# Conditioning projections in four column groups; the linear attention's two directions issued in pairs

## The chip, the cores and the metric

The kernel runs on one core of one Trainium2 chip. The metric is device time of one execution in microseconds. The kernel before took 5521.72 us as the median of three runs (5514.61 to 5526.49).

## The reference

One inference step of a two-layer backbone of width 1024, for 128 context tokens and 512 latent tokens. Each layer has a token mixer and then an expert channel mixer, and each of these is modulated by vectors that come from a conditioning vector:

```
mod = silu(cond) @ ada_w + ada_b            # (2 conditionings, 6 * 1024): shift1, scale1, gate1, shift2, scale2, gate2
h   = x * (1 + scale1) + shift1
x   = layer_norm(ALPHA * x + gate1 * token_mixer(h))
h   = x * (1 + scale2) + shift2
x   = layer_norm(ALPHA * x + gate2 * peer(h))
```

The token mixer runs grouped attention beside a gated linear attention, which scans the tokens in chunks of 64, once forward and once backward, in four heads, with a 128 x 256 state S:

```
def step(S, inp):                            # one chunk of one direction of one head
    o     = A @ v + q_e @ S                  # 64 x 256
    S_new = exp(b_last) * S + (k * exp(b_last - b)).T @ v
```

The context has two chunks and starts from zero states, the latents have eight and start from given ones. The expert mixer (`peer`) picks 128 of 16384 rows of two tables for each token by product keys.

## The kernel before, in words

One core does everything. The program is written as Python generators that trace instructions; `merge` and `weave` interleave two tracks by hand-written costs: the latent track (`s_mixer(0)`, `s_peer(0)`, `s_mixer(1)`, `s_peer(1)`) and the context track (`p_mixer`, `p_front`, `p_peer` for each layer). The framework's planner then fixes the order of the instructions on each engine when the program is built: it takes the traced order as priority and simulates when operands and buffers come free. On the chip each engine follows its fixed order and waits on semaphores; all plain transfers of weights are issued by SP, the expert gathers by GpSimd.

*Conditioning.* `ada(l, vs, W)` makes the vectors `vs` of layer l for both conditionings at once. It is called three times: alone at the very start for shift1 and scale1 of layer 0 (`p_ada(0)`); inside the context mixer of layer 0 for the other four (`mixer`, with the mixer's own four weight buffers); and for all six vectors of layer 1 (`p_ada(1)`) woven with the context gathers of layer 0. The weights of one vector are 1024 x 1024. They are read in four column tiles of 256 columns, each in two transfers of 512 KB (`Weights.__call__`, line 129). For each tile, eight products of fp32, `csil` (128 x 2, stationary) with 128 x 256 weights (moving), accumulate in rows 0 and 1 of a PSUM tile `modr` (line 151); each product is two matmul instructions. Then VectorE copies `modr` to `mr` (line 169), and two transposes (line 161) turn `mr` into columns of `modp`, one tile later. PSUM has two banks under the tag `mm0`, of which `modp` holds one for a whole vector and `modr` the other. `p_ada(0)` has 12 weight buffers of 512 KB, `p_ada(1)` has 2. After the first two tiles `p_ada` calls `layer_params`, which issues small transfers.

*Linear attention.* `gates(h)` prepares the operands of head h, `scan(h)` runs its two directions. In each step the loop of lines 454 to 474 goes through direction 0 and then direction 1, each in its own chunk: the product with the state, `o` (line 461: stationary 128 rows x 64 columns, so 64 of the array's columns, in the half that the chunk's place decides); the state's increment, `kv` (line 466: stationary 64 rows x 128 columns, so 64 of the array's rows, in the half that the chunk's place decides), into one of two PSUM banks (`mm0` for the context, `mm1` for the latents); and the update of S on VectorE (line 471, or 469 where S was zero). Since the step's two chunks are n and last - n, the two directions always use opposite halves. The latents' last step has no `kv`, the context's first step no `o`.

Of the kernel before, what the change touches and what calls it, by code (L numbers as in the profile page):

```python
# [7 lines left out]
F32 = mybir.dt.float32  # L8
# [10 lines left out]
L = 2  # L19
D = 1024  # L20
ND = D // 128
SP, SS, PAST = 128, 512, 256
H, G, HD = 16, 4, 64
GH, DK, DV = 4, 128, 256
# [7 lines left out]
CW = 256  # L32
# [31 lines left out]
def kernel(ctx: ExitStack, tc, xp, xs, ck, cv, st, cond, adaw, adab, win, wglr,  # L64
                              nrm, w2, gb, gn, wao, wgo, wout, lnp, wq, sk, pu, put, pv, rope, cst, msk,
                              yp, ys, nk_out, nv_out, ns_out):
    nc = tc.nc
# [23 lines left out]
    def psm(name, tr=0):  # L91
        return ps.tile([128, 512], F32, tag=f"mm{tr}", bufs=2, name=name)
# [21 lines left out]
    csil = consts.tile([128, ND, 2], F32, name="csil")  # L114
# [6 lines left out]
    class Weights:  # L121
        def __init__(self, pool_, split, bufs):
            self.pool, self.split, self.bufs = pool_, split, bufs

        def __call__(self, src):
            raw, h, lo = [], [], []
            for i in range(2):
                r = self.pool.tile([128, 4, CW], F32, tag="w", bufs=self.bufs, name="w")
                nc.sync.dma_start(r, src[:, 4 * i:4 * i + 4, :])
                raw.append(r)  # L130
                if not self.split:
                    continue
                wh = self.pool.tile([128, 4, CW], F32R, tag="wh", bufs=3, name="wh")
                nc.scalar.activation(wh, r, AF.Copy)  # L134
                wl = self.pool.tile([128, 4, CW], F32R, tag="wl", bufs=3, name="wl")
                (nc.vector, nc.gpsimd)[i].tensor_sub(wl, r, f32(wh))  # L136
                h.append(wh)
                lo.append(wl)
            if not self.split:
                return [lambda j: raw[j // 4][:, j % 4, :]]  # L140
            return [lambda j: h[j // 4][:, j % 4, :], lambda j: lo[j // 4][:, j % 4, :]]
# [6 lines left out]
    def accumulate(out, mk):  # L148
        n = len(mk)
        for i, (lt, rt) in enumerate(mk):  # L150
            nc.tensor.matmul(out, lt, rt, start=(i == 0), stop=(i == n - 1))  # L151

    def ada(l, vs, W):
        p = lp[l]
        for v in vs:
            mp = psm("modp")
            m3 = mp[:, 0:2 * ND].rearrange("p (c s) -> p c s", s=2)

            def turn(t, mr):
                for k in range(2):  # L160
                    nc.tensor.transpose(m3[:, 2 * t + k, :], mr[:, k * 128:(k + 1) * 128], ident[0:2, 0:2])

            late = None
            for t in range(4):
                w = W(adaw[l, 4 * v + t])
                rp = psm("modr")
                accumulate(rp[0:2, 0:CW], [(csil[:, j, :], w[0](j)) for j in range(ND)])
                mr = lay.tile([2, CW], F32, tag="mr", bufs=2, name="mr")
                nc.vector.tensor_copy(mr, rp[0:2, 0:CW])
                if late:  # L170
                    turn(*late)
                late = t, mr
                yield 3.5
            turn(*late)
            mod = lay.tile([128, ND, 2], F32, tag=f"mod{v}", bufs=2, name="mod")
            nc.vector.tensor_add(mod, m3, p["adb"][:, ND * v:ND * v + ND, None].to_broadcast([128, ND, 2]))
            if v in (SCALE1, SCALE2):
                nc.vector.tensor_scalar(mod, mod, 1.0, None, op0=OP.add)
            elif v == GATE1:
                nc.vector.tensor_scalar(mod, mod, 0.5, None, op0=OP.mult)  # L180
            p["mod", v] = mod
            if v in (SHIFT1, SCALE1):
                continue
            rp = psm("rowp")
            nc.tensor.transpose(rp[0:2 * ND, 0:128], mod.rearrange("p c s -> p (c s)"), ident)
            rows = lay.tile([2 * ND, 128], F32, tag="rows", bufs=2, name="rows")
            nc.vector.tensor_copy(rows, rp[0:2 * ND, 0:128])
            rowd = dram.tile([2 * ND, 128], F32, name=f"rowd{l}{v}")
            nc.sync.dma_start(rowd, rows)
            p["row", v] = rowd  # L190
        yield 0.5
# [57 lines left out]
    def mixer(tr, l, W):  # L249
# [69 lines left out]
        with mkp("ld") as ld:  # L319
            for b in (ROWS + DENSE if tr and l else range(nb)):  # L320
# [4 lines left out]
                v = ld.tile([128, ND, 128], F32, tag="v", bufs=2, name="v") if split else hT[0]  # L325
# [18 lines left out]
        with mkp("gla") as gl:  # L344
# [17 lines left out]
            t = psm("glr", tr)  # L362
# [66 lines left out]
            def scan(h):  # L429
# [23 lines left out]
                        nc.sync.dma_start(S[d], st[l, d, h])  # L453
                for n_ in range(ncb):
                    last = n_ == ncb - 1
                    for d in range(2):
                        cc = (n_, ncb - 1 - n_)[d]
                        b, hf = divmod(cc, 2)
                        pr_ = slice(hf * 64, hf * 64 + 64)
                        if S[d] is not None:  # L460
                            nc.tensor.matmul(o[pr_, b * DV:(b + 1) * DV], a_[d][:, cc * CH:(cc + 1) * CH], S[d],
                                             start=False, stop=False, skip_group_check=True)
                        if last and tr == 1:
                            continue
                        kv = psm("kv", tr)
                        nc.tensor.matmul(kv[:, 0:DV], ks_[d][pr_, b, :], gv[pr_, b, :], start=True, stop=True)
                        S2 = gl.tile([128, DV], F32, tag=f"S{d}", bufs=2 + tr, name="S")
                        if S[d] is None:
                            nc.vector.tensor_copy(S2, kv[:, 0:DV])
                        else:  # L470
                            nc.vector.scalar_tensor_tensor(S2, S[d], ee_[d][:, cc:cc + 1], kv[:, 0:DV],
                                                           op0=OP.mult, op1=OP.add)
                        S[d] = S2
                    yield 1.8
# [654 lines left out]
    def take(g, n):  # L1129
        for _ in range(n):  # L1130
            yield next(g)
# [48 lines left out]
    def p_ada(l):  # L1180
        with ExitStack() as st_:
            lp[l] = {}
            vs = (SHIFT1, SCALE1) if l == 0 else (SHIFT1, SCALE1, GATE1, SCALE2, SHIFT2, GATE2)
            g = ada(l, vs, Weights(opener(st_, 0)("wa"), False, (AB, 2)[l]))
            yield from take(g, 2)
            layer_params(l)
            if l == 0:
                nc.sync.dma_start(iota, cst[:, 128 + SS:128 + SS + NC])
                wide = sm.tile([128, NK], F32, tag="wk", bufs=2, name="wide")
                nc.sync.dma_start(wide, cst[:, 128 + SS:256 + SS])  # L1190
                nc.vector.tensor_copy(keys, wide)
            yield from g
# [45 lines left out]
def _layout(i):  # L1238
# [3 lines left out]
    def wtiles(w):  # L1242
        n = w.shape[-1] // CW
        return np.ascontiguousarray(w.reshape(L, ND, 128, n, CW).transpose(0, 3, 2, 1, 4))
# [4 lines left out]
    o = {}  # L1249
# [2 lines left out]
    o["cv"] = a["cache_v"][0].reshape(L, PAST, G * HD)  # L1252
    o["st"] = a["state_gla"][0]
    o["cond"] = np.ascontiguousarray(np.stack([cols(a["c"][0]), cols(a["c_ctx"])], axis=-1))
    o["adaw"] = wtiles(a["ada_w"])
    o["adab"] = cols(a["ada_b"])
    w = a["w_in"]
    sp = np.cumsum([0, 1024, 256, 256, 512, 512, 1024, 1024, 32, 2048])
# [56 lines left out]
```

## Time and profile before

| | us |
|---|---|
| median of three runs | 5521.72 |
| lowest, highest run | 5514.61, 5526.49 |
| the profiled execution | 5526.76 |
| its span, first to last instruction | 5525.0 |

| engine | busy us | share of the span |
|---|---|---|
| TensorE matmul (PE) | 4570.1 | 83% |
| TensorE weight load (PEld) | 3388.7 | 61% |
| VectorE (DVE) | 3905.2 | 71% |
| ScalarE (ACT) | 1041.1 | 19% |
| GpSimd (POOL) | 2251.5 | 41% |

All durations come from the one profiled execution. A busy share is a union of the engine's instructions over a stretch; a stage's limit is read from its own stretch, not from this table. "Granted clock" is the mean share of TensorE's full clock in a stretch. In a timeline, a row with xN merges N instructions of one line that follow each other; the bracket says how long the engine was idle before and what ended it. Matmul rows overlap at their ends: the distance between two starts is the time that the first one holds the engine. The first 43 us are the conditioning alone; 43 to some 700 us hold the context mixer and the first part of the latent one; 800 to 1350 us the context gathers beside the latents' attention; from some 1520 us on the latent expert stage; 3080 us starts layer 1's latent mixer.

### The profile page before, as it was taken

What the parts mean: (1) busy time and instruction counts of PE and PEld (TensorE: products, weight loads), DVE (VectorE), ACT (ScalarE), POOL (GpSimd) and SP (SyncE); (2) the same over time, 40 slices, a digit from 0 to 9 for tenths busy, and PEclk for the clock granted to TensorE, in tenths of its full rate; (3) what the DMA queues carried; (4) which work ended last, traced back from release to release, by engine and by line L of the source; (5) the groups of instructions that cost most, each with busy time, mean ns of one, the idle gap of its engine ahead of it and who ended that gap; (6) DMA issues with size and microseconds to landing.
All of it is one profiled execution on the core that took longest, in us unless ns stands there. A gap on an engine that the chain in (4) does not pass through costs nothing.

```text
span 5525.0 us, 71758 instructions
## 1 busy us (share of the span) xinstructions
PE 4570.1 (83%) x26668; PEld 3388.7 (61%) x26668; DVE 3905.2 (71%) x8024; ACT 1041.1 (19%) x1860; POOL 2251.5 (41%) x1652
## 2 busy tenths in 40 slices
PE   8879988877776789799999668689877458998998
PEld 5658665655655566467774445578776347675743
DVE  4342368887499996967656798864248999978682
ACT  4231123322211201010000222145221010000000
POOL 0000017675355552343441476620135656245450
PEclk9979998988887799899999778788988679998999
DMA  5325558998388888799996688830447889698995
GB/s 180 117 69 176 190 183 320 318 327 304 135 311 322 326 310 314 249 352 342 369 364 236 215 305 290 300 112 19 133 135 258 323 313 356 214 397 302 409 331 204
DMA packets 472735, 1440.71 MB, mean 261 GB/s; under 512 B 55232, under 2 KB 123968, under 8 KB 472384
## 3 DMA queue, kind: packets, MB, share of 16 engines
q0 software_dynamic: 221184, 805.40, 39.9%
q1 hardware_dynamic: 251200, 630.71, 32.4%
q8 instruction: 209, 3.42, 0.2%
q14 instruction: 142, 1.16, 0.1%
HBM read 1391.29 MB, written 44.63 MB: 260 GB/s over the span
## 4 chain that ended last, share of the span: by engine, by line
DVE 16%; PE 16%; issue 8%; DMA 7%; POOL 2%; ACT 1%; another core or an unknown queue 1%; SPq 0%; DVEq 0%; POOLq 0%; ACTq 0%
DMA gat<-in_pv,idx 4%; PE vacc L1083 4%; DVE gat L904 4%; PE gt L151 3%; DVE acc L934 3%; DMA gat<-in_pu,idx 2%; PE proj L151 2%; PE po L151 2%; POOL gat L887 1%; PE hp L151 1%; DVE A L1042 1%; PE qp L151 1%; DVE Q L1062 1%; DVE bw L1050 1%; PE pTp L626 1%
## 5 line engine op out<-in xcount | busy, mean ns | idle before, releaser
L887 POOL DMA_INDIRECT gat<-in_pu,idx x768 | 991.9, 1292 | 886.8 <-DVE gat L904 382.2
L887 POOL DMA_INDIRECT gat<-in_pv,idx x768 | 962.7, 1253 | 789.4 <-DVE acc L934 468.0
L934 DVE SCALAR_TENSOR_TENSOR acc<-gat,dots,acc 128x1024 f32<-128x1024 f32 x762 | 999.0, 1311 | 155.8 <-DMA gat<-in_pv,idx 141.4
L904 DVE SCALAR_TENSOR_TENSOR gat<-gat,h 128x1024 f32<-128x1024 f32 x768 | 945.1, 1242 | 141.4 <-DMA gat<-in_pu,idx 129.8
L151 PE MATMUL hp<-h2Td,uc 128*128 128x256 f32 x4096 | 947.9, 392 | 76.3 <-DVE wk L787 48.9
L1083 PE MATMUL vacc<-v,Q 128*128 128x512 f32 x2048 | 925.2, 605 | 14.3 <-DMA v<-in_pv 13.6
L151 PEld LDWEIGHTS hp<-h2Td,uc 128*128 128x128 f32 x4096 | 799.3, 197 | 199.7 <-DVE wk L787 52.2
L136 POOL TENSOR_TENSOR wl<-w,wh 128x1024 fp32r<-128x1024 f32 x92 | 232.0, 2521 | 1447.2 <-ACT wh L134 1358.1
L1083 PEld LDWEIGHTS vacc<-v,Q 128*128 128x128 f32 x2048 | 384.7, 193 | 456.5 <-issue 437.0
L134 ACT ACTIVATE wh<-w 128x1024 fp32r<-128x1024 f32 x184 | 194.2, 1057 | 706.4 <-PE proj L151 282.7
L996 ACT ACTIVATE Q<-hp 128x512 f32<-128x512 f32 x128 | 76.4, 597 | 1117.0 <-PE hp L151 1022.7
L151 PE MATMUL proj<-wh,hTh 128*128 128x256 f32 x896 | 264.1, 295 | 7.2 <-DVE sgo L486 3.4
L151 PE MATMUL proj<-wl,hTh 128*128 128x256 f32 x896 | 262.0, 292 | 5.5 <-POOL wl L136 5.5
L151 PE MATMUL proj<-wh,hTl 128*128 128x256 f32 x896 | 263.7, 294 | 0.0
L1057 PEld LDWEIGHTS <-A 128*128 128x128 bf16 x6144 | 174.6, 96 | 132.5 <-issue 61.7
L136 DVE TENSOR_TENSOR wl<-w,wh 128x1024 fp32r<-128x1024 f32 x92 | 127.8, 1389 | 173.6 <-ACT wh L134 163.4
L1057 PE MATMUL Gp<-bw,A 128*128 128x32 bf16 x6144 | 181.0, 177 | 77.4 <-DVE bw L1050 57.3
L151 PE MATMUL po<-V,pT 128*128 128x64 f32 x1600 | 220.0, 279 | 10.2 <-ACT pT L628 8.4
L151 PEld LDWEIGHTS po<-V,pT 128*128 128x128 f32 x1600 | 211.1, 201 | 20.0 <-ACT pT L628 12.7
L151 PE MATMUL modr<-w,csil 128*2 128x256 f32 x768 | 193.9, 405 | 21.4 <-DMA w<-in_adaw 17.7
L618 DVE TENSOR_REDUCE nm<-s 128x1 f32<-128x768 f32 (+1 forms) x160 | 130.9, 819 | 114.0 <-PE s L151 112.7
L151 PEld LDWEIGHTS proj<-wh,hTh 128*128 128x128 f32 x896 | 176.1, 197 | 18.1 <-issue 13.2
(297 smaller groups left out, 7567.1 us busy)
## 6 DMA issues: line engine op xcount, KB each, us to landing
uc<-in_put SPq DMA_DIRECT2D x256, 512.0 KB
v<-in_pv SPq DMA_DIRECT2D x256, 512.0 KB
w<-in_win SPq DMA_DIRECT2D x208, 512.0 KB
w<-in_adaw SPq DMA_DIRECT2D x96, 512.0 KB
w<-in_wq SPq DMA_DIRECT2D x64, 512.0 KB
w<-in_wgo SPq DMA_DIRECT2D x32, 512.0 KB
w<-in_wao SPq DMA_DIRECT2D x32, 512.0 KB
w<-in_wout SPq DMA_DIRECT2D x32, 512.0 KB
```

Source lines behind the costliest of these rows:

```text
L134: nc.scalar.activation(wh, r, AF.Copy)
L136: (nc.vector, nc.gpsimd)[i].tensor_sub(wl, r, f32(wh))
L151: nc.tensor.matmul(out, lt, rt, start=(i == 0), stop=(i == n - 1))
L618: nc.vector.tensor_reduce(nm, s[:, 0:KEYS], axis=AX.X, op=OP.max, negate=True)
L626: nc.tensor.transpose(t[:, (kc - c0) * 128:(kc - c0 + 1) * 128], pr[:, kc * 128:(kc + 1) * 128], ident)
L887: i = nc.gpsimd.indirect_dma_start(out=t, out_offset=None, in_=src, in_offset=bass.IndirectOffsetOnAxis(ap=self.res[b][0][:, k:k + 1], axi ...
L904: nc.vector.scalar_tensor_tensor(u, u, 1.0, h2, op0=OP.mult, op1=OP.mult, accum_out=dots[:, k:k + 1])
L934: nc.vector.scalar_tensor_tensor(acc, v, w_, acc, op0=OP.mult, op1=OP.add)
L996: nc.scalar.activation(q[:, i:i + 2, :].rearrange("p i t -> p (i t)"), t, AF.Gelu_apprx_tanh)
L1042: nc.vector.tensor_tensor(a.rearrange("p t (i w) -> p t i w", w=2), pairs[:, None].to_broadcast([128, TG, NK // 2, 2]), i1[:, sl, None, :] ...
L1057: nc.tensor.matmul(t[:, j * CI:(j + 1) * CI], a[:, j, :], bw[:, j, q, :], start=(q == 0), stop=(q == 2))
L1083: nc.tensor.matmul(accs[i][:, s * 512:(s + 1) * 512], w[:, j, i * 128:(i + 1) * 128], v[:, s * 512:(s + 1) * 512], start=(key == 0), stop= ...
```

## The change

`ada` reads the weights of a vector in eight slabs of 128 rows x 1024 columns (512 KB each, laid out anew on the host before the launch) in place of four column tiles. For each slab it issues four products, one for each quarter of the columns, with the same `csil` columns; the four results go to partitions 0, 32, 64 and 96 of one PSUM tile, that is, to four groups of 32 columns of the array. After the eighth slab four copies (`evac`, ScalarE and VectorE in turn) and their transposes follow. `p_ada` calls `layer_params` after four slabs (2 MB, as before).

In the scan, a step issues `kv` of both directions first, then `o` of both, then the two updates of S; both `kv` banks are taken at once.

```diff
--- before.py
+++ after.py
@@ -122,6 +122,11 @@
         def __init__(self, pool_, split, bufs):
             self.pool, self.split, self.bufs = pool_, split, bufs
 
+        def slab(self, src):
+            r = self.pool.tile([128, 4 * CW], F32, tag="w", bufs=self.bufs, name="w")
+            nc.sync.dma_start(r, src)
+            return r
+
         def __call__(self, src):
             raw, h, lo = [], [], []
             for i in range(2):
@@ -160,18 +165,17 @@
                 for k in range(2):
                     nc.tensor.transpose(m3[:, 2 * t + k, :], mr[:, k * 128:(k + 1) * 128], ident[0:2, 0:2])
 
-            late = None
-            for t in range(4):
-                w = W(adaw[l, 4 * v + t])
-                rp = psm("modr")
-                accumulate(rp[0:2, 0:CW], [(csil[:, j, :], w[0](j)) for j in range(ND)])
+            rp = psm("modr")
+            for j in range(ND):
+                w = W.slab(adaw[l, v, j])
+                for q in range(4):
+                    nc.tensor.matmul(rp[32 * q:32 * q + 2, 0:CW], csil[:, j, :], w[:, q * CW:(q + 1) * CW],
+                                     start=(j == 0), stop=(j == ND - 1))
+                yield 1.75
+            for q in range(4):
                 mr = lay.tile([2, CW], F32, tag="mr", bufs=2, name="mr")
-                nc.vector.tensor_copy(mr, rp[0:2, 0:CW])
-                if late:
-                    turn(*late)
-                late = t, mr
-                yield 3.5
-            turn(*late)
+                evac(mr, rp[32 * q:32 * q + 2, 0:CW])
+                turn(q, mr)
             mod = lay.tile([128, ND, 2], F32, tag=f"mod{v}", bufs=2, name="mod")
             nc.vector.tensor_add(mod, m3, p["adb"][:, ND * v:ND * v + ND, None].to_broadcast([128, ND, 2]))
             if v in (SCALE1, SCALE2):
@@ -453,22 +457,29 @@
                         nc.sync.dma_start(S[d], st[l, d, h])
                 for n_ in range(ncb):
                     last = n_ == ncb - 1
+                    at_ = []
                     for d in range(2):
                         cc = (n_, ncb - 1 - n_)[d]
                         b, hf = divmod(cc, 2)
-                        pr_ = slice(hf * 64, hf * 64 + 64)
+                        at_.append((d, cc, b, slice(hf * 64, hf * 64 + 64)))
+                    kv = {}
+                    if not (last and tr == 1):
+                        for d, cc, b, pr_ in at_:
+                            kv[d] = psm("kv", tr)
+                        for d, cc, b, pr_ in at_:
+                            nc.tensor.matmul(kv[d][:, 0:DV], ks_[d][pr_, b, :], gv[pr_, b, :], start=True, stop=True)
+                    for d, cc, b, pr_ in at_:
                         if S[d] is not None:
                             nc.tensor.matmul(o[pr_, b * DV:(b + 1) * DV], a_[d][:, cc * CH:(cc + 1) * CH], S[d],
                                              start=False, stop=False, skip_group_check=True)
-                        if last and tr == 1:
+                    for d, cc, b, pr_ in at_:
+                        if d not in kv:
                             continue
-                        kv = psm("kv", tr)
-                        nc.tensor.matmul(kv[:, 0:DV], ks_[d][pr_, b, :], gv[pr_, b, :], start=True, stop=True)
                         S2 = gl.tile([128, DV], F32, tag=f"S{d}", bufs=2 + tr, name="S")
                         if S[d] is None:
-                            nc.vector.tensor_copy(S2, kv[:, 0:DV])
+                            nc.vector.tensor_copy(S2, kv[d][:, 0:DV])
                         else:
-                            nc.vector.scalar_tensor_tensor(S2, S[d], ee_[d][:, cc:cc + 1], kv[:, 0:DV],
+                            nc.vector.scalar_tensor_tensor(S2, S[d], ee_[d][:, cc:cc + 1], kv[d][:, 0:DV],
                                                            op0=OP.mult, op1=OP.add)
                         S[d] = S2
                     yield 1.8
@@ -1182,7 +1193,7 @@
             lp[l] = {}
             vs = (SHIFT1, SCALE1) if l == 0 else (SHIFT1, SCALE1, GATE1, SCALE2, SHIFT2, GATE2)
             g = ada(l, vs, Weights(opener(st_, 0)("wa"), False, (AB, 2)[l]))
-            yield from take(g, 2)
+            yield from take(g, 4)
             layer_params(l)
             if l == 0:
                 nc.sync.dma_start(iota, cst[:, 128 + SS:128 + SS + NC])
@@ -1252,7 +1263,7 @@
     o["cv"] = a["cache_v"][0].reshape(L, PAST, G * HD)
     o["st"] = a["state_gla"][0]
     o["cond"] = np.ascontiguousarray(np.stack([cols(a["c"][0]), cols(a["c_ctx"])], axis=-1))
-    o["adaw"] = wtiles(a["ada_w"])
+    o["adaw"] = np.ascontiguousarray(a["ada_w"].reshape(L, ND, 128, 6, D).transpose(0, 3, 1, 2, 4))
     o["adab"] = cols(a["ada_b"])
     w = a["w_in"]
     sp = np.cumsum([0, 1024, 256, 256, 512, 512, 1024, 1024, 32, 2048])
```

## Rows read from the trace of the kernel before

**Rows 1.** Busy us (instructions) per engine, granted clock, DMA share, GB/s, by stretch.

```profile
0.00:43.00 43.00, 33.82 (x160) 13.95 (x160) 8.29 (x18) 4.67 (x5) 2.55 (x5) 1.00 0.88 315
43.00:480.00 437.00, 375.77 (x1948) 284.17 (x1949) 172.44 (x466) 162.17 (x334) 27.47 (x10) 0.90 0.30 100
480.00:700.00 220.00, 201.09 (x1288) 147.15 (x1287) 73.11 (x185) 27.51 (x49) 17.44 (x7) 0.96 0.62 205
800.00:1110.00 310.00, 263.95 (x1562) 178.54 (x1561) 262.01 (x529) 97.52 (x202) 212.15 (x143) 0.90 0.90 322
1110.00:1350.00 240.00, 174.31 (x769) 136.21 (x769) 207.39 (x179) 58.23 (x93) 173.32 (x125) 0.84 0.93 336
1150.00:1200.00 50.00, 25.27 (x80) 17.44 (x78) 41.08 (x34) 8.24 (x12) 37.53 (x28) 0.69 0.96 343
1350.00:1520.00 170.00, 133.66 (x746) 116.31 (x745) 88.41 (x112) 41.59 (x46) 53.49 (x19) 0.88 0.40 138
3080.00:3620.00 540.00, 368.28 (x1877) 279.10 (x1878) 490.10 (x801) 139.93 (x218) 363.72 (x267) 0.77 0.83 287
```

**Rows 2.** The same view of the instructions on `modr` alone (PE, PEld, DVE).

```profile
0.00:43.00 43.00, 30.01 (x128) 10.67 (x128) 3.29 (x8) 1.00 0.88 315
480.00:700.00 220.00, 57.84 (x256) 20.42 (x256) 6.58 (x16) 0.96 0.62 205
800.00:1110.00 310.00, 97.62 (x353) 28.65 (x352) 9.37 (x23) 0.90 0.90 322
```

**Rows 3.** Timeline of the start: start, us, engine, line, idle before.

```profile
38.17 3.62 PE L151 MATMUL modr<-w,csil 128*2 128x256 f32 x16 [0.64 <-DVE mr L169]
...
41.82 0.41 DVE L169 COPY mr<-modr 2x256 f32<-2x256 f32 x1 [0.41 <-PE modr L151]
...
43.09 3.62 ACT L336 ACTIVATE v<-xt,mod 128x128 f32<-128x128 f32 x8 [4.02 <-DVE mod L178]
```

**Rows 4.** Stretches of the start, DMA share and GB/s last.

```profile
0.00:10.00 10.00, 3.64 (x11) 1.21 (x12) 0.35 (x2) 1.50 (x2) 0.20 (x4) 1.00 0.73 237
10.00:20.00 10.00, 9.42 (x46) 3.64 (x45) 1.63 (x5) 0.00 (x0) 0.00 (x0) 1.00 0.88 308
20.00:30.00 10.00, 9.71 (x48) 3.88 (x46) 1.00 (x3) 0.00 (x0) 0.00 (x0) 1.00 1.02 401
```

**Rows 5.** The page's DMA issues: transfer, queue, count, KB each.

```profile
w<-in_adaw SPq DMA_DIRECT2D x96, 512.0 KB
```

**Rows 6.** Timeline of TensorE in two scans' steps.

```profile
132.25 1.13 PE L466 MATMUL kv<-gv,ks 64*128 64x256 f32 x4
133.30 0.39 PE L151 MATMUL proj<-wh,hTl 128*128 128x256 f32 x1
...
141.29 0.65 PE L461 MATMUL o<-S,a 128*64 128x256 f32 x4
141.88 0.70 PE L466 MATMUL kv<-gv,ks 64*128 64x256 f32 x2
142.50 0.65 PE L461 MATMUL o<-S,a 128*64 128x256 f32 x2
```

**Rows 7.** Timeline of TensorE around one column tile.

```profile
541.78 3.62 PE L151 MATMUL modr<-w,csil 128*2 128x256 f32 x16
545.33 0.39 PE L151 MATMUL proj<-wl,hTh 128*128 128x256 f32 x1
```

**Rows 8.** PE and PEld busy, 43 to 480 us, lines 461, then 466.

```profile
43.00:480.00 437.00, 35.28 (x112) 10.44 (x112) 0.90 0.30 100
...
43.00:480.00 437.00, 40.43 (x116) 17.37 (x116) 0.90 0.30 100
```

**Rows 9.** What TensorE waited for, 800 to 1110 us: us, times, longest.

```profile
PE s L626 <- ACT pr L620: 16.1, 12, 2.5
PE modr L151 <- DMA w<-in_adaw: 8.5, 3, 3.4
PE s L626 <- ACT pT L628: 5.0, 8, 0.7
```

## The prediction, as put on record before the change ran

> **What bounds the kernel now.** I read the table by stage first [rows 1], because no engine is the limit throughout. Up to 43 us only the first two conditioning vectors are made: DMA share 0.88, TensorE busy 33.8 of 43 us. From 43 to 480 us (the latent mixer's linear attention beside the context mixer) TensorE is busy 376 of 437 us and DMA 0.30. From 480 to 700 us, which holds the other four vectors of layer 0, TensorE is busy 201 of 220 us and everything else is under two thirds: TensorE is the limit there. From 800 to 1350 us the context expert gathers run: DMA 0.90 and 0.93, VectorE 262 of 310 us, TensorE 264 of 310 us. From 1350 to 1520 us the latent mixer finishes alone (DMA 0.40), and the latent expert stage starts behind it. From 3080 to 3620 us (layer 1's linear attention beside the second gathers) VectorE is busy 490 of 540 us and TensorE 368.
>
> Then the operations touched. The conditioning matmuls (`modr`) take 30.0, 57.8 and 97.6 us of TensorE in three stretches [rows 2], for 8, 16 and 22 of 24 column tiles (16 instructions each). At the start TensorE and not DMA ends that stage: `modr` of the last tile waits for the copy `mr`, starts at 38.17 us, and the first use of the finished vector, `v`, starts at 43.09 us [rows 3]. By then DMA had long delivered: 10 us at 237, 308 and 401 GB/s are 9.5 MB by 30 us [rows 4].
>
> **Conditioning: the price of a slab.** Now: a tile of 16 matmul instructions holds TensorE from 541.78 to 545.33 us, 3.55 us, or 0.22 us each [rows 7]. New: two slabs, each with four products into four column groups, two instructions per product. Four groups are not in the trace, but two halves of the columns are: the two `o` products of a scan's first step, which stand together by chance, are four instructions from 141.29 to 141.88 us, 0.59 us; one `o` product alone, two instructions, runs from 142.50 us and its row is 0.65 us long too, against 0.65 us for the four [rows 6]. So two column groups run fully beside each other, and an fp32 product's second half does not hold up the other group. I take 0.61 us for a slab. Bounds: 1.2 us if only two groups overlap (twice 0.59), and 1.8 us if none do (8 times 0.22).
>
> [...]
>
> **Conditioning: what it is worth by place.**
> - *Start, 8 tiles.* TensorE work falls from 30 us to 16 times 0.61, 10 us, and DMA becomes the limit: 16 slabs of 512 KB [rows 5] with some 1 MB queued between them (small parameters, one input block) are 9.4 MB, landed at 30 us by [rows 4]. Four copies now stand together at a vector's end, two on VectorE and two on ScalarE (0.41 us each, [rows 3]), with transposes behind each; I put 3 us for tail and addition, so `v` at 33 us instead of 43.09. The input blocks behind it must land too and DMA is nearly full, so I take 8.5 us. Bounds 0 (inputs and first weights are late anyway) and 12.
> - *Layer 0's other four vectors, 16 tiles.* 16 times 3.55 is 57 us, 32 times 0.61 is 19.5 us: 37 us less TensorE work in a stretch that has 19 us of idleness [rows 1]. Each slab must be loaded within four buffers: 32 slabs at 401 GB/s are 42 us, below the some 180 us that this stretch would still last, so DMA does not take over. Behind this comes a normalisation on VectorE that TensorE waits for. I take 30. Bounds 8 (slabs arrive late) and 37.
> - *Layer 1's six vectors, 24 tiles.* They cost 97.6/22, 4.4 us each and 106 us in all; the granted clock is 0.90 there. 48 slabs at 0.61 times 4.4/3.6 are 36 us: 70 us less, 64 of them between 800 and 1110 us. But here the matmuls partly fill holes: TensorE still waits 16.1 and 5.0 us for the softmax's ScalarE steps [rows 9], and with the filler smaller these waits grow. The gathers cannot be faster than DMA: 0.90 of 310 us leaves 31 us. The latent mixer that ends at 1520 us can use the rest, since VectorE has 557 us of work in the 720 us from 800 on and TensorE 572 [rows 1]. I take 25. Bounds 0 and 64.
>
> [...]
>
> Copies: 48 on VectorE become 24 there and 24 on ScalarE; the vector's end is a new wait for TensorE's transposes, behind which the attention's matmuls stand, but 12 such ends replace 48 waits for the single `modr` buffer. The number of SP transfers stays 96, of the same size; rewriting the weights' layout is done before the launch.
>
> **The linear attention.** A step is two directions of one `o` (0.59 us, as 64 columns) and one `kv` (141.88 to 142.50, 0.62 us, as 64 rows) [rows 6]. If the two `o` stand together they save 0.59 a step, as shown. The `kv` pair in opposite row halves is not in the trace. Nearest row: two `kv` that follow each other, 132.25 to 133.30 us, 1.05 us against 1.24 alone [rows 6]. [...] By the loops layer 0 has 36 pairs of each; the 112 and 116 instructions of [rows 8], four to a pair, are 28 and 29 of them. 36 times 0.59 plus 36 times 0.19 to 0.62 is 28 to 43 us of TensorE at most. But each product waits for VectorE's update of its own direction, and the updates come one after the other, so a pair will often be split, and TensorE is only 86% busy there. I take 13; bounds 0 and 30, and minus 5 if both `kv` banks held at once delay others. Layer 1: VectorE sets the pace (490 of 540 us); I take 4, bounds minus 5 and 15.
>
> **Sum.** 8.5 + 30 + 25 + 13 + 4 = 80.5 us. The profiled execution took 5526.8 us (span 5525.0), 5.0 above the median of the three runs: 5446 against it, 5441 against the median. Everything after 1520 us (latent experts, layer 1) only moves ahead.
>
> **Rivals** (measurement can tell about 0.2%, 11 us, from no change):
> - *The freed time is slack.* The gathers' DMA and VectorE hold the stage to 1350 us, and the mixers' chains refill with waiting. [...] Against: 480 to 700 us is TensorE's alone. 8.5 us at the start and some 10 us elsewhere: 5503. Chance 0.13.
> - *Four groups overlap only two by two.* A slab costs 1.2 us: 37 falls to 18, 70 to 36. 8 + 15 + 13 + 17: 5469. Against: nothing in the two-half rows hints at a limit. Chance 0.08.
> - [...] Chance 0.04.
> - *Slower: late slabs.* With two buffers in layer 1, each slab's matmuls stand in TensorE's program order until their own 512 KB have landed, while DMA is 0.9 busy, and the attention's matmuls stand behind it. Before, this wait was 8.5 us in three cases [rows 9]. 48 waits of 3 us are 144 us, against a gain of 80: 5585. It decides from 1.7 us a slab. Against: 310 us hold 44 slabs, 7 us each, and a slab needs DMA for 1.3 to 1.6 us. Chance 0.09.
>
> **Chances and range.** Forecast 0.66. Its own spread reaches from 5385 (nearly all bounds, 140 us) to 5495. The range 5385 to 5508 takes in the half-overlap case and most of the slack case; left out are the late slabs, no overlap, and a little below. Faster: 0.65 from the forecast, 0.08, and 0.09 of the slack case, 0.82. Same: 0.07. Slower: 0.09 from late slabs and 0.02 without overlap, 0.11.
>
> **What would show it.** `modr` in one slab: eight instructions within some 0.6 us at full clock, and `modr`'s busy time under 80 us in all. `v`'s first start near 33 us. The first context gather some 50 us earlier; the latent mixer's end 75 us earlier. `o` in rows of four within 0.65 us; `kv` in rows of four at 0.7 or at 1.1 us. Wrong if `modr` waits for `in_adaw` beyond 30 us in all, if starts of a slab's second group lie 0.2 us behind the first's, or if TensorE's idle time before 1520 us grows by as much as its work shrinks.

## The result, and the profile after

| | before | after |
|---|---|---|
| median, first comparison (four runs each) | 5524.1 | 5435.05 (5426.14 to 5452.28) |
| ratio, 95% interval | | 0.9844 (0.9821 to 0.9868) |
| median, second comparison, another chip (15 and 4 runs) | 5503.53 | 5427.9 |
| ratio, 95% interval | | 0.9853 (0.9837 to 0.9868) |
| the profiled execution | 5526.76 | 5433.52 |

The change makes the kernel 1.5% faster; 5441 us had been forecast. The stretches of the kernel after, cut roughly at the same work as the stretches of [rows 1] (columns as there; lengths between the same two events stand in the table by stage below):

```profile
0.00:38.00 38.00, 18.40 (x160) 5.98 (x160) 6.22 (x12) 5.11 (x8) 2.54 (x5) 0.97 0.92 335
38.00:470.00 432.00, 374.83 (x1975) 283.35 (x1976) 171.46 (x469) 155.84 (x331) 24.95 (x10) 0.90 0.32 103
470.00:657.00 187.00, 174.58 (x1330) 140.59 (x1329) 76.96 (x189) 38.59 (x74) 17.61 (x7) 0.95 0.72 241
...
752.00:1060.00 308.00, 251.06 (x1642) 196.42 (x1635) 260.28 (x517) 106.83 (x225) 184.42 (x142) 0.76 0.89 318
1060.00:1300.00 240.00, 174.93 (x715) 136.38 (x715) 203.49 (x172) 53.37 (x78) 174.25 (x129) 0.82 0.94 342
1300.00:1457.00 157.00, 121.58 (x690) 106.01 (x689) 89.07 (x109) 37.33 (x42) 48.13 (x17) 0.87 0.42 142
```

The start is 5 us shorter, the stretch of layer 0's other vectors 33 (27 between the same two events), the one after the gathers 13. The 308 us from 752 us on are as long as the 310 of before, and there the granted clock fell from 0.90 to 0.76.

`modr` alone, against [rows 2], in the three stretches: 14.11, 18.17 and 40.55 us, 72.8 in all, where 193.9 were (185.5 in the stretches of [rows 2], the rest between 700 and 800 us):

```profile
0.00:43.00 43.00, 14.11 (x128) 2.42 (x128) 1.68 (x4) 1.50 (x4) 0.91 0.92 330
470.00:660.00 190.00, 18.17 (x256) 4.24 (x256) 3.33 (x8) 3.01 (x8) 0.96 0.72 242
700.00:1110.00 410.00, 40.55 (x384) 5.96 (x384) 4.96 (x12) 4.50 (x12) 0.79 0.83 293
```

Three slabs in a row, against the column tile of [rows 7]: 24 instructions hold TensorE from 579.85 to 581.26 us, 0.47 us a slab.

```profile
579.85 1.48 PE L172 MATMUL modr<-w,csil 128*2 128x256 f32 x24
581.26 0.39 PE L156 MATMUL proj<-wl,hTh 128*128 128x256 f32 x1
```

Within a slab the trace has four instructions starting at 0, 7, 14 and 20 ns and the other four at 215, 222, 229 and 235 ns; the records do not name the column group, and one instruction of each group in each four is the reading that fits. A slab that stands alone holds the engine for 0.545 us.

The end of the first stage, against [rows 3]:

```profile
29.41 0.61 PE L172 MATMUL modr<-w,csil 128*2 128x256 f32 x8 [0.67 <-DMA w<-in_adaw]
30.16 0.37 ACT L100 ACTIVATE mr<-modr 2x256 f32<-2x256 f32 x1 [9.03 <-PE modr L172]
...
30.79 1.09 PE L333 MATMUL xt<-ident,x 128*128 128x128 f32 x8
...
32.20 0.42 DVE L104 COPY mr<-modr 2x256 f32<-2x256 f32 x1 [1.23 <-PE modp L166]
33.17 0.20 PEld L166 LDWEIGHTS modp<-ident,mr 2*128 2x128 f32 x2 [0.17 <-issue]
...
34.31 1.23 DVE L141 TENSOR_TENSOR wl<-w,wh 128x1024 fp32r<-128x1024 f32 x1 [1.69 <-ACT wh L139]
...
35.57 0.17 DVE L180 TENSOR_TENSOR mod<-modp,adb 128x16 f32<-128x16 f32 x1
35.66 2.34 POOL L141 TENSOR_TENSOR wl<-w,wh 128x1024 fp32r<-128x1024 f32 x1 [35.21 <-ACT wh L139]
35.78 2.25 DVE L182 TENSOR_SCALAR mod<-mod 128x16 f32<-128x16 f32 x1
...
38.12 0.81 ACT L340 ACTIVATE v<-xt,mod 128x128 f32<-128x128 f32 x2 [2.54 <-DVE mod L182]
```

The scan's steps, against [rows 6], first step and second, then a later one:

```profile
140.47 0.70 PE L470 MATMUL kv<-gv,ks 64*128 64x256 f32 x2
141.09 0.65 PE L473 MATMUL o<-S,a 128*64 128x256 f32 x4
141.67 0.70 PE L470 MATMUL kv<-gv,ks 64*128 64x256 f32 x2
142.30 0.65 PE L473 MATMUL o<-S,a 128*64 128x256 f32 x2
...
175.29 0.70 PE L470 MATMUL kv<-gv,ks 64*128 64x256 f32 x4
175.92 0.65 PE L473 MATMUL o<-S,a 128*64 128x256 f32 x2
```

The pair at 175.29 us is the only `kv` pair that runs fully side by side (0.63 us for four instructions). Of the 144 `o` products 106 stand alone as runs of two instructions, 20 in ten runs of four and 18 in six runs of six (before 120 alone and 24 in fours); 10 of the 72 pairs start together, where 7 did before.

What TensorE waited for from 752 to 1060 us (us, times, longest), against [rows 9]: the softmax's waits grew from 21.1 to 27.8 us, the one for slabs by 0.9 us. Up to 1600 us `modr` waited for `in_adaw` 26.2 us in 23 places: 13.7 us at the start, 1.9 in the stretch of layer 0's other vectors and 10.6 (9 places) for layer 1's.

```profile
PE s L637 <- ACT pr L631: 18.4, 15, 2.6
PE s L637 <- ACT pT L639: 9.4, 13, 0.9
PE modr L172 <- DMA w<-in_adaw: 9.4, 7, 2.1
```

**Where TensorE's time went.** Up to the first `qp` of the latents, at 1499.4 us before and 1436.7 us after, both kernels run the same 7092 matmul instructions. All of them, then `modr`, `po` and `s` alone (`s` holds the attention's scores, `po` its weighted values), of the kernel before:

```profile
0.00:1499.40 1499.40, 1253.56 (x7092) 942.60 (x7092) 869.50 (x1731) 420.68 (x793) 486.39 (x309) 0.90 0.61 212
...
0.00:1499.40 1499.40, 193.90 (x768) 62.38 (x768) 19.63 (x48) 0.90 0.61 212
...
0.00:1499.40 1499.40, 110.19 (x800) 104.23 (x800) 8.35 (x20) 0.90 0.61 212
...
0.00:1499.40 1499.40, 144.43 (x688) 97.85 (x688) 65.36 (x80) 133.99 (x304) 0.90 0.61 212
```

The same four of the kernel after:

```profile
0.00:1436.70 1436.70, 1177.98 (x7092) 927.45 (x7092) 863.32 (x1708) 422.72 (x813) 451.88 (x309) 0.87 0.64 222
...
0.00:1436.70 1436.70, 72.84 (x768) 12.61 (x768) 9.97 (x24) 9.01 (x24) 0.87 0.64 222
...
0.00:1436.70 1436.70, 130.79 (x800) 125.82 (x800) 8.39 (x20) 0.87 0.64 222
...
0.00:1436.70 1436.70, 163.81 (x688) 110.09 (x688) 65.37 (x80) 134.65 (x304) 0.87 0.64 222
```

`modr` gave 121 us back, but TensorE's work fell by 76 us only: `po` grew by 20.6 us and `s` by 19.4 us, with the same instructions. Of the 800 `po` matmuls 52 took more than 350 ns before and 247 after; most of the others take 275 ns or less and the long ones mostly 421 ns. What changed around them is the granted clock, 0.76 in place of 0.90 in the gathers' first stretch, a mixture of 0.50 and 1.00, the only two shares of the full clock in the clock records of these two traces. The records show that this is the cause: all 52 long ones of before lie wholly in stretches at 0.50, and so do 245 of the 247 of after (one of them by 97%). In after, the 48 that start within 753 to 789 us, at 0.50, take 421 ns in the median, the 192 within 1022.5 to 1097 us, at 1.00, 275 ns.

The other profiles bear it out. Up to the latents' first `qp`, `po` and `s` together take 253 to 258 us in the four kernels with 180 to 194 us of `modr` (before among them), 265 in l0_only (`modr` 133), 270 in two_groups (112), and 281 to 297 in the seven profiles with 68 to 74 us of `modr`. So the 40 us are the first pair's; 27 to 42 is what the seven show against before.

**By stage.** Stage lengths by the first or last start of an operation, us (`v` is the modulated input of a mixer, `gt` its gate, `qp` the expert stage's queries). The columns: to the first `v`; on to layer 0's first `gt` of the context; on to its last `modr`; on to the latents' last `gt` in layer 0 (layer 1's vectors lie here); layer 1's first `v` to its latents' first `gt`; all the rest of the profiled span. The ratio is that of the timed runs.

| kernel | start | scan 0 | four vectors | six vectors | scan 1 | rest | ratio to before |
|---|---|---|---|---|---|---|---|
| before | 43.1 | 413.9 | 197.3 | 754.3 | 787.5 | 3329 | |
| after | 38.1 | 408.5 | 170.4 | 728.9 | 777.4 | 3308 | 0.9844 |
| after_again | 38.0 | 409.4 | 172.3 | 728.5 | 783.2 | 3308 | 0.9853 |
| start_only | 38.2 | 413.7 | 197.9 | 756.9 | 786.7 | 3313 | 1.0006 |
| l0_only | 37.9 | 413.3 | 171.5 | 751.0 | 791.5 | 3304 | 0.9949 |
| cond_only | 38.4 | 414.2 | 171.1 | 724.1 | 794.9 | 3316 | 0.9903 |
| scan_only | 43.8 | 407.3 | 192.6 | 756.8 | 780.8 | 3307 | 0.9997 |
| two_groups | 34.6 | 412.8 | 180.4 | 721.8 | 788.0 | 3304 | 0.9888 |
| after_yield | 38.1 | 407.6 | 170.3 | 727.9 | 793.7 | 3321 | 0.9885 |
| ab4 | 38.5 | 408.1 | 170.3 | 739.0 | 783.5 | 3309 | 0.9909 |
| forced | 38.5 | 399.9 | 164.0 | 701.7 | 776.9 | 3302 | 0.9792 |
| forced_yield | 39.1 | 399.7 | 165.5 | 712.5 | 779.8 | 3307 | 0.9823 |
| forced_scan | 43.4 | 409.8 | 190.5 | 749.5 | 778.5 | 3305 | 0.9956 |

Of what these kernels change, the rest holds only the context's linear attention of layer 1, 8 of that layer's 36 `kv` pairs. It varies from 3302 to 3321 us among the experiments, and 20 of the 93 us between the two first profiled executions lie there; what makes it vary was not found. The five stages of the change gave 73 us.

Each row is one execution; forced_ab4 has none, as its profiled execution was a slow one (13138 us). The same kernel twice (after, after_again) differs by at most 2 us in the first four stages and by 6 in scan 1. Two stages separate the kernels by far more than that: the four vectors' stage takes 190 to 198 us with column tiles and 170 to 172 with slabs in four groups and the pairs not ordered; the six vectors' takes 750 to 757 with tiles, and 722 to 729 with slabs, two buffers and the pairs not ordered.

### The profile page after: what moved, and what is told of

Its sections match the earlier page's. It is cut to its first block, busy times and chain, and to the rows that moved or that the text cites. A ratio compares the mean times of both kernels' runs of the same rounds, so it can differ in the third digit from the quotient of the medians.

```text
span 5431.7 us, 71674 instructions
## 1 busy us (share of the span) xinstructions
PE 4484.3 (83%) x26668; PEld 3366.8 (62%) x26668; DVE 3900.9 (72%) x8000; ACT 1037.8 (19%) x1876; POOL 2226.8 (41%) x1652
## 4 chain that ended last, share of the span: by engine, by line
PE 42%; DVE 26%; DMA 14%; issue 12%; POOL 3%; ACT 2%; SPq 0%; DVEq 0%; another core or an unknown queue 0%; POOLq 0%; ACTq 0%
PE vacc L1094 8%; PE proj L156 7%; PE gt L156 7%; DVE gat L915 6%; DMA gat<-in_pv,idx 6%; PE hp L156 6%; DMA gat<-in_pu,idx 4%; DVE acc L945 3%; PE po L156 3%; POOL gat L898 3%; PE qp L156 2%; DVE A L1053 1%; DVE Q L1073 1%; PE s L156 1%; PE gqk L156 1%
## 5 line engine op out<-in xcount | busy, mean ns | idle before, releaser
L898 POOL DMA_INDIRECT gat<-in_pu,idx x768 | 969.1, 1262 | 898.4 <-DVE gat L915 407.3
L141 POOL TENSOR_TENSOR wl<-w,wh 128x1024 fp32r<-128x1024 f32 x92 | 228.6, 2485 | 1339.3 <-ACT wh L139 1094.7
L156 PE MATMUL po<-V,pT 128*128 128x64 f32 x1600 | 239.8, 297 | 13.1 <-ACT pT L639 8.0
L156 PEld LDWEIGHTS po<-V,pT 128*128 128x128 f32 x1600 | 232.5, 220 | 24.8 <-ACT pT L639 13.2
L141 DVE TENSOR_TENSOR wl<-w,wh 128x1024 fp32r<-128x1024 f32 x92 | 123.4, 1341 | 164.8 <-ACT wh L139 154.5
L156 PEld LDWEIGHTS proj<-wl,hTh 128*128 128x128 f32 x896 | 175.3, 196 | 20.7 <-issue 13.8
```

What stands on the lines that cost most here:

```text
L898: i = nc.gpsimd.indirect_dma_start(out=t, out_offset=None, in_=src, in_offset=bass.IndirectOffsetOnAxis(ap=self.res[b][0][:, k:k + 1], axi ...
```

## The experiments

All were timed against the kernel before in five rounds; before took 5505.4, 5503.5 and 5508.0 us (medians) in the three groups, which ran on different chips.

**The parts alone.** *cond_only*: the conditioning changed, the scan's loop as before. *scan_only*: the reverse.

> The conditioning in column groups, the linear attention's order of issue as in the kernel before. The theory: nearly all of the gain is the conditioning's, since in the changed kernel's trace the pairs of the scan stand almost nowhere side by side (its first linear attention gains about 1.5 us); so 5444 us, within 12 us, some 80 us faster than before. The rival: the reordering of the scan brings a real part, 25 us or more, which would leave this kernel at 5465 us or above.

> The linear attention's order of issue alone, the conditioning as before. The theory: 0 to 15 us faster than before, about 5515 us, with the contexts of the two linear attentions some 2 to 10 us earlier. The rival, that the pairs bring 25 us or more: about 5495 us or below.

Measured: 5454.06 us, 0.9903 (0.9886 to 0.9919), and 5497.05 us, 0.9997 (0.9986 to 1.0009). The scan's order alone is worth nothing that can be told from no change (2 us by the ratio, 8 by the two medians), within the theory's 0 to 15; the conditioning alone gave 53 us and not 80.

*after_again*: the changed kernel itself, unedited.

> The changed kernel itself, beside kernels that hold parts of it. Measured apart, the conditioning alone gave a ratio of 0.9903 and the scan's order alone 0.9997; the two together had given 0.9844 on another chip. If the parts add up, this one comes to about 0.990 (5450 us against 5505 us); if the scan's order gains only where the conditioning has been changed too, to about 0.984 (some 5420 us).

0.9853: the first comparison is confirmed, and the parts (53 and 2 us) do not add up to the 81.

**The conditioning by place.** *l0_only* keeps column tiles for layer 1, *start_only* for all but the first two vectors; both have the scan as before and the old copies with the old tiles (shortened, against the kernel after):

```diff
-            rp = psm("modr")
-            for j in range(ND):
+            if l == 0:                  # start_only: l == 0 and v < 2
+                rp = psm("modr")
+                for j in range(ND):
...
+            else:
+                late = None
+                for t in range(4):
...
```

> Column groups in layer 0's conditioning alone; layer 1's six vectors are multiplied in column tiles as before, and the scan is as before. The theory: layer 1's vectors, beside the first expert stage's transfers, are worth 14 to 25 us, so this kernel stands that much above the one with column groups in both layers, at about 5462 us. The rival: TensorE's time freed there is slack, since the stage is paced by the gathers of the experts' weights; then both stand at about 5444 us.

> Column groups for the first two vectors of layer 0 alone (the start); all others are multiplied in column tiles as before, and the scan is as before. The theory: the start is worth 5 to 9 us (5497 to 5500 us against 5505 us), and the other four vectors of layer 0, beside the linear attention's end and the context's projections, the remaining 20 us or so of the 28 us that layer 0's column groups gave. The rival: layer 0's gain is the start and its longer cover of the scan; then this kernel already shows 20 us or more.

Measured: 5477.28 us, 0.9949 (0.9930 to 0.9967), and 5506.6 us, 1.0006 (0.9995 to 1.0016). The start was expected to bring 5 to 9 us: it ends 5 us earlier in the trace, but the time does not show it; what takes it back is not settled. Layer 0's other four vectors (l0_only against start_only, on two chips) are worth 0.0057, some 31 us (26 in their own stage), and layer 1's six (cond_only against l0_only) 0.0046, some 25 us, 11 to 39 by the two intervals (27 in their own stage). The rival that TensorE's time freed in layer 1 is slack falls, by the stage above all.

**Half the concurrency.** *two_groups*:

```diff
-                for q in range(4):
-                    nc.tensor.matmul(rp[32 * q:32 * q + 2, 0:CW], csil[:, j, :], w[:, q * CW:(q + 1) * CW],
+                for q in range(2):
+                    nc.tensor.matmul(rp[32 * q:32 * q + 2, 0:2 * CW], csil[:, j, :], w[:, 2 * q * CW:2 * (q + 1) * CW],
...
-                evac(mr, rp[32 * q:32 * q + 2, 0:CW])
+                evac(mr, rp[32 * (q // 2):32 * (q // 2) + 2, q % 2 * CW:(q % 2 + 1) * CW])
```

> The changed kernel with two column groups in place of four, each over 512 columns (four instructions a slab, of twice the length): the same slabs, copies and transposes, half the concurrency. The theory: a slab holds TensorE for 0.95 to 1.0 us in place of 0.545, so the 96 slabs take some 40 us more of it; the conditioning gave 53 us for about 121 us of TensorE's time (cond_only), so 15 to 25 us are lost against the changed kernel: a ratio of 0.988 to 0.990. The rival: TensorE's time is not what counts, but the layout of the slabs (one set of copies and transposes for each vector, at its end): then within 5 us of the changed kernel, 0.985 to 0.986.

Measured: 5443.84 us, 0.9888 (0.9867 to 0.9909), where the theory had put it. Four slabs, 16 instructions, and then `modr`, `po` and `s` up to the latents' first `qp`, in this kernel:

```profile
561.31 3.60 PE L172 MATMUL modr<-w,csil 128*2 128x512 f32 x16
564.84 0.38 PE L156 MATMUL proj<-wh,hTh 128*128 128x256 f32 x1
```

```profile
0.00:1440.50 1440.50, 111.76 (x384) 11.92 (x384) 9.89 (x24) 8.96 (x24) 0.88 0.64 221
...
0.00:1440.50 1440.50, 115.98 (x800) 111.39 (x800) 8.37 (x20) 0.88 0.64 221
...
0.00:1440.50 1440.50, 154.27 (x688) 103.38 (x688) 65.24 (x80) 134.17 (x304) 0.88 0.64 221
```

A slab costs 0.88 us in a row (0.96 alone), `modr` 39 us more than after. But `po` and `s` are 24 us shorter, and the stage of the six vectors is no longer than in the changed kernel (721.8 against 728.5 us); the loss that a stage shows lies where TensorE is the limit, in the four vectors' stage (10 us, for 13 us more `modr` there). So the last halving of the slab's price brings nothing beside the gathers. The time alone would not decide it: after_yield below, which changes only an order, lands at the same ratio.

**The pairs, ordered.** *forced*: both `o` may be issued only behind the second `kv`. *forced_scan*: the same on scan_only.

```diff
-                            nc.tensor.matmul(kv[d][:, 0:DV], ...)
-                    for d, cc, b, pr_ in at_:
+                            kvi = nc.tensor.matmul(kv[d][:, 0:DV], ...)
+                    with tc.issue_after(kvi.ins) if kv else nullcontext():
+                        for d, cc, b, pr_ in at_:
```

> The changed kernel, with the products that read the state (both directions) ordered behind the second state update's matmul on TensorE, so that the pairs really form. The theory: the pairs failed only because the planner issues each direction as it comes ready; so the matmuls of the state go in fours that hold TensorE for about 0.63 us and the reading ones in fours of about 0.58 us, for about 1.13 + 0.65 us twice before, the scan gets shorter by several us per layer, and the time is 10 to 20 us below the changed kernel's (5415 to 5425 us). The rival: the scan is paced by VectorE's state updates, one direction after the other, and TensorE now stands still until the later direction is ready: 5435 to 5450 us, no gain over the changed kernel or a loss.

> The ordered pairs of the scan on the kernel before, its conditioning unchanged. The theory: the two linear attentions get 10 to 20 us shorter together, as the traces of the ordered pairs show against those of the unordered, so 0.996 to 0.998 against before (0.9997 for the unordered order). The rival: 30 us or more, 0.9945 or below, as the step from 0.985 to 0.979 would have it.

Measured: 5389.28 us, 0.9792 (0.9774 to 0.9811), and 5479.62 us, 0.9956 (0.9941 to 0.9972). Against after_again forced gained 34 us, more than the theory's 10 to 20; forced_scan lies just below its theory's 0.996, with an interval that reaches both theories. In the trace of forced 55 runs of four and 6 of eight hold 67 of the 72 `o` pairs:

```profile
160.85 0.70 PE L470 MATMUL kv<-gv,ks 64*128 64x256 f32 x2
161.48 0.65 PE L474 MATMUL o<-S,a 128*64 128x256 f32 x4
162.06 0.49 PE L443 MATMUL A<-a,en 128*128 128x128 f32 x2
162.48 0.70 PE L470 MATMUL kv<-gv,ks 64*128 64x256 f32 x2
```

The `kv` stay mostly single (95 of 144 products). In layer 0 `o` takes 48.4 us of TensorE in place of 63.0, and scan 0 is 9 us shorter than in after. More is gained later, in the six vectors' stage (27 us), where no scan runs; here the first 143 us from the first gather on, of after_again and of forced:

```profile
757.00:900.00 143.00, 109.79 (x685) 83.07 (x683) 120.66 (x253) 40.88 (x86) 83.10 (x65) 0.69 0.89 317
```

```profile
739.00:882.00 143.00, 119.75 (x799) 95.04 (x792) 120.93 (x264) 49.26 (x105) 88.72 (x64) 0.75 0.88 322
```

Forced runs 114 matmul instructions more there, at a clock of 0.75 in place of 0.69. Why its plan is better filled in that stretch was not tried. On the old conditioning the ordering shortens neither scan stage by more than 3 us (409.8 and 778.5 us in forced_scan, 407.3 and 780.8 in scan_only), so where its gain lies there is open.

**How much is the packing?** *after_yield* and *forced_yield* are controls in which the planner is only told another price for a slab:

```diff
-                yield 1.75
+                yield 1.5
```

> A control: the changed kernel with the same instructions, but the planner told that a slab costs 1.5 instead of 1.75, so that only the order of the interleaving changes. If the 25 us by which four buffers made the changed kernel slower, and by which the parts fail to add up, come from the buffers and the scan, this stays within 5 us of the changed kernel (ratio 0.984 to 0.986). The rival: such differences are made by how the stage beside the gathers happens to be packed; then this one moves by 10 us or more, either way.

> The same control on the kernel with the ordered pairs (0.9792 before). The theory: of its gain over the changed kernel some 15 us are the scan's and hold under any packing, the rest (a tail of the latent mixer of 21 us after the last gather, 52 us in the changed kernel) is packing; so the ratio lies at 0.979 to 0.984. The rival: the whole gain is the pairs', 0.978 to 0.980.

Measured: after_yield 5444.79 us, 0.9885 (0.9865 to 0.9905), forced_yield 5405.45 us, 0.9823 (0.9803 to 0.9844). The same work in another order costs 0.3%, some 17 us, in both; since the ratios come from different chips and their intervals meet, the size is rough, and that it is there at all rests on the two agreeing. The rival is borne out in size: a difference of that size in the time of two kernels here says nothing about an edit. It is not borne out in place: in after_yield the stage beside the gathers is as long as in the changed kernel (727.9 against 728.9 us), while scan 1 and the rest are 16 and some 12 us longer (in forced_yield 11 of 21 us do lie beside the gathers). The 26 us by which the parts fail to add up are little more, and lie likewise: against after, cond_only is 18 us longer in scan 1, 8 in the rest and 6 in scan 0, and 5 shorter beside the gathers. Pair by pair, though, the kernels with ordered pairs stand below their counterparts every time: by 0.0061 and 0.0062 (after_again, after_yield), 0.0047 (ab4) and 0.0041 (scan_only), 23 to 34 us.

**Late slabs.** *ab4*, and *forced_ab4* (the same edit on forced):

```diff
-            g = ada(l, vs, Weights(opener(st_, 0)("wa"), False, (AB, 2)[l]))
+            g = ada(l, vs, Weights(opener(st_, 0)("wa"), False, (AB, 4)[l]))
```

> The changed kernel with four buffers in place of two for layer 1's slabs. The changed kernel's matmuls of the slabs wait 26 us for the slabs' transfers up to 1600 us. The theory: these waits lie in a stage that the transfers pace, beside other waits, so they go down but the time stays within 5 us of the changed kernel's. The rival: late slabs cost what they show, and the time falls by up to 26 us.

> The ordered pairs of the scan together with four buffers for layer 1's slabs. The theory: the ordered pairs' gain stays whole and the buffers add at most 5 us: a ratio of 0.979 against the kernel before, as with the ordered pairs alone (0.9792). The rival: the buffers add 15 us or more: 0.976 or below.

Measured: 5454.39 us, 0.9909 (0.9895 to 0.9923), and 5428.2 us, 0.9862 (0.9847 to 0.9877): slower by 0.0056 and 0.0070 than after_again and forced, which neither theory had. The slabs of layer 1 in the trace (instructions, ns, first and last start), of after_again and then of ab4:

```profile
L172 PE MATMUL modr<-w,csil x384: 377/513/634, 744.1 to 1035.2; 128*2 128x256 f32 x192
```

```profile
L172 PE MATMUL modr<-w,csil x384: 377/379/634, 745.9 to 924.6; 128*2 128x256 f32 x192
```

With four buffers the slabs are through 111 us earlier, in the stretch in which TensorE has the attention beside them, and are missing later: the stage is 10.5 us longer. The two profiled executions differ by 9 us and the medians by 26; how much of that is packing is open. TensorE's wait for the softmax's `pr` is 33.6 us there, 18.4 in after_again (757 to 1356 us), which fits the missing filler. But the buffers did not take the waits for slabs away, as both theories had assumed: up to 1600 us they are 26.5 us in ab4 and 27.7 in after_again. So what these waits cost stays unmeasured; shown is that two more buffers do not remove them, and that using the slabs up earlier does not pay.

## Why the prediction was right, and where not

- **The price of a slab** (0.61 us taken, bounds 1.2 and 1.8): 0.545 alone, 0.47 in a row of three. The second instruction, the second group's by the reading above, starts 7 ns behind the first. Overlap two by two only and no overlap at all are both ruled out. Each further slab in a row adds 0.43 us, so a slab that stands alone costs 0.11 us more than one behind another.
- **Layer 0's other four vectors** (30): 27 us in their stage between before and after, 26 between l0_only and start_only, 31 in the time, for 40 us less `modr` there. Right, and for the reason given: TensorE was the limit there [rows 1].
- **Layer 1's six vectors** (25 of at most 70): 25 us in their stage in the first pair, 25 in the time between cond_only and l0_only, for 66 us less `modr` there. The size is right, its reason half. [rows 9] had been read as holes that would grow. They did, by little: TensorE's idle time up to the latents' `qp` went from 246 to 259 us. Some 40 us went into the same attention matmuls, which got longer at the lower clock: a cost for which the sum had no term. The granted clock fell from 0.90 to 0.76 there; what makes it fall was not shown. With the packing it moves too: from 757 to 1060 us it is 0.76 in after_again (TensorE busy 244 us), 0.81 in after_yield with the same work (239 us), and 0.84 in two_groups with 21 us more `modr` (248 us).
- **Start** (8.5; `v` at 33 us): 5.0 in the trace, `v` at 38.12 us. The slabs had landed by 29.4 us as worked out, but the tail takes 8.7 us, not 3: the copies take turns with transposes of the inputs, an `L141` subtraction slips in ahead of the addition `L180`, and the adding of 1 to scale1 behind it (`L182`), 0.17 us in two_groups, takes 2.25 us. It ends 0.03 us behind GpSimd's subtraction beside it (35.66 to 38.00 us). Two more of these operations, at 556.95 and 578.06 us, take 2.11 and 1.53 us and also end 0.03 us behind a subtraction of GpSimd, while the addition `L180` at 556.74 and 577.85 us, beside the same subtractions, takes 0.17 us. That GpSimd's subtraction holds these operations up is the author's reading of these rows; by what, they do not show. In two_groups, where GpSimd's subtraction comes later, `v` starts at 34.65 us:

```profile
34.17 0.17 DVE L180 TENSOR_TENSOR mod<-modp,adb 128x16 f32<-128x16 f32 x1 [0.92 <-PE modp L166]
34.38 0.17 DVE L182 TENSOR_SCALAR mod<-mod 128x16 f32<-128x16 f32 x1
...
34.65 0.81 ACT L340 ACTIVATE v<-xt,mod 128x128 f32<-128x128 f32 x2 [1.07 <-DVE mod L182]
```

- **The linear attention** (13 and 4): 5.4 us in scan 0 and 10 in scan 1 of the first pair, 6 and 6 between scan_only and start_only, and nothing measurable in the time; the 10 cannot be held to be the pairs', since after_yield's scan 1 is 16 us longer than after's with the same instructions. For a `kv` pair 0.19 (1.24 less 1.05) to 0.62 us had been put down, from [rows 6]; the one pair fully side by side took 0.63 us, so it saved 0.61. The step that failed is "a pair will often be split": taken as a discount, it was nearly the rule (10 of 72 `o` pairs start together). A state's update comes one direction after the other, and the planner issues what comes ready first. Ordered, they bring 23 to 34 us in the time, inside the two bounds of 30 and 15 added up; but of the 49 us between the profiled executions of after and forced 9 lie in scan 0, 6 in the four vectors' stage, which holds the last head's scan, and under 1 in scan 1, so most of that is not the saving that was meant.
- **The sum** (80.5): 73 us in the stages of the change and 20 us in the rest, for which nothing had been forecast; 86 and 81 us by the two ratios. The terms that were too large and the 20 us of the rest cancel, so that the total came within 6 us is in part luck.
- **Late slabs**: `modr` waited 26.2 us for `in_adaw`, under the 30 named. Of these 10.6 us fall on layer 1's 48 slabs, 0.2 us a slab, far below the 1.7 us from which that rival decides; the 24 tiles of before had waited 11.4 us.
- The signs named: the first gather 48.6 us earlier (50 said), the latents' first `qp` 62.7 us earlier (75 said for the mixer's end), `modr` 72.8 us in all (under 80). TensorE's idle time grew by 13 us while its work shrank by 76, far from the sign of being wrong.

## What to carry to other kernels

A product with two stationary columns leaves unused 126 of the 128 that other products in these traces fill (128*128); four such products in four column groups cost hardly more than one (0.47 us a slab in a row, where one product took 0.44). Of the time saved on the engine about two thirds came off the kernel's time where TensorE is the limit (27 of 40 us), and some 40% where the products only fill gaps (25 of 66 us): other matmuls there got slower, and waits grew. Issuing two products next to each other in the program does not place them next to each other on the engine: where they must stand together, order them, and look at the timeline for runs of four. Before an edit of 20 us is believed, the same kernel in another packing is the control, and the lengths of the stages say more than the total.

## What the runs showed that was not expected

- Removing 121 us of matmuls from an engine lengthened others, unchanged, by 40 us, and the granted clock of their stretch fell from 0.90 to 0.76; with two groups (39 us more `modr`) they were 24 us shorter again. Nearly all the long `po` matmuls (245 of 247) lie in stretches at the lower clock.
- A 0.17 us VectorE operation took 2.25 us beside a GpSimd operation of 2.34 us, and two more of them 2.11 and 1.53 us.
- The eight instructions of four fp32 products in four groups run in two waves (starts at 0, 7, 14, 20 ns, then 215 to 235 ns), and two 64-row `kv` in opposite halves take 0.63 us together, as long as one.
- Four slab buffers in place of two made both kernels slower, by 0.0056 and 0.0070; the filler was used up 111 us earlier, and the waits for slabs stayed.
